# One weight ring for both phases of the FFNs and the mixing, with w2 in pieces of four feature blocks

## The chip, the cores and the metric

The kernel runs on one core of a Trainium2 chip. The metric is the device time of one execution in microseconds (us), as the median of several runs. The engines are TensorE (PE: matmuls, PEld: weight loads), VectorE (DVE), ScalarE (ACT), GpSimd (POOL) and SyncE (SP, which here issues nearly all DMAs).

## The reference, cut to what matters

One layer of a decoder trunk over 1104 tokens (16 meta, 1024 prompt, 64 sample) of width 1024, with a feed-forward width of 2816:

```python
def swiglu(x, w1, w3, w2):
    return (jax.nn.silu(x @ w1) * (x @ w3)) @ w2

x = x + 0.5 * swiglu(rmsnorm(x, ffn1_norm_g), ffn1_w1, ffn1_w3, ffn1_w2)
y, st = mix(rmsnorm(x, mix_norm_g), state, params)      # w_in, three recurrences, w_out
x = x + y
x = x + 0.5 * swiglu(rmsnorm(x, ffn2_norm_g), ffn2_w1, ffn2_w3, ffn2_w2)
out = rmsnorm(x, final_norm_g)
```

All is float32.

## The kernel before, in words

Every float32 operand of a matmul is split into a high part (a cast to a rounded float32 form, on ScalarE, L114) and a low part (the rest, on VectorE, L115). A product is three matmuls: high by high, high by low, low by high. Activations lie with features on the partitions, in 128-wide feature blocks, and tokens along the free axis. The helper that makes the two parts is `split`.

The program has these stages, in time order. FFN1, first phase (0 to 521 us): `group` (matmul L355) and `plain` (matmul L403) make the 22 blocks of the hidden vector from w1 and w3. Weights come as 128x4x256 raw tiles (`raw`, two buffers, pool r1, 4 KB a partition each) and as seven pairs of `whi` and `wlo` of 512 elements (pool w1). A finished hidden tile goes to DRAM (L413, L437). FFN1, second phase (521 to 825 us): the loop over THIRDS1 takes the tokens in three thirds of 336, 384 and 384 columns; for each it reads x into `xo` (L1567, one buffer), reads the 22 hidden blocks of those columns back (`hr`, L472, three buffers; the first third's come from tiles read earlier) and calls `third`. `third` runs over four pairs of output blocks and, inside, over pieces of w2: it loads a piece (L487), splits it, does its matmuls (L493) and at the end of a pair adds the result to x (L500). Pieces are of three feature blocks, the last two of two; raw, high and low tiles of w2 have two buffers each in a pool of their own. The mixing (825 to 1347 us): weights of w_in and w_out come through `wload` (load L188, matmul L198) in a pool "wp" of three buffers each for raw, high and low, 1024 elements at a time, 28 units; around them run the recurrences. The third block of w_out and the norms of FFN2 (1347 to 1420 us), where `wfetch` (L1620) loads w_out and L1638 multiplies. FFN2, first phase (1420 to 1899 us), as in FFN1. FFN2, second phase (1909 to 2180 us): the loop over THIRDS2, thirds of 320, 384 and 384 columns, with x from L1696 and w2 in pieces of 6, 6, 5 and 5 blocks (KQ). Then the last outputs are written.

The order on each engine and queue is set ahead of time by a scheduler that simulates the program; each engine and each DMA queue then works strictly in that order. Tiles rotate within their pools: a tile can be written when the last reader of the tile before it in the same buffer is done, and a pool's memory can be used by a later pool when its readers are done.

While the second phase of FFN1 begins, SP also issues the loads of the constants of the mixing (L1358 to L1447: wif, wtml, st, wkS, wvS, wqS and others) and the first loads of the mixing's weights.

## Time and profile before

| what | value |
|---|---|
| median of 3 runs | 2199.27 us (2198.92 to 2201.39) |
| the profiled execution | 2197.51 us, its span 2195.8 us |
| TensorE busy | 2091.2 us, 95% of the span |
| VectorE, ScalarE, GpSimd busy | 59%, 41%, 13% |
| mean granted TensorE clock | 0.977 |
| DMA | 275.47 MB, mean 125 GB/s |

The span is the time from the first to the last instruction that the profiler records. A granted clock of 1.00 is 2.4 GHz, 0.5 is 1.2 GHz. In a timeline a row that ends in [a <-b] had its engine idle for a us before it, and b is what ended that. The chain of work that ended last is followed back from the last instruction, and each of its pieces is what the next one waited for.

### The profile page before, as it was taken

The page shows a single profiled execution, that of the slowest core. Times are in us where ns is not written, and L with a number is a line of the kernel's source. Part 1 is how long each engine was busy: PE and PEld are TensorE (multiplying, and loading weights), DVE is VectorE, ACT ScalarE, POOL GpSimd, SP SyncE. Part 2 cuts the span into 40 slices and gives each one's busy share as a digit, 9 for nine tenths or more (in the row PEclk, how much of TensorE's full clock was granted, in tenths as well). Part 3 has the DMA queues.
Part 4 walks back from the last instruction along what each step waited for, and adds up shares of the span by engine and source line. Part 5 has one row for each costly group of instructions (what it writes and reads, how often), then busy time and mean ns, then how long its engine had stood idle before and what let it go on. Part 6 is the DMA issues. An engine that isn't in the chain of part 4 may idle for free.

```text
span 2195.8 us, 37582 instructions
## 1 busy us (share of the span) xinstructions
PE 2091.2 (95%) x14600; PEld 2040.3 (93%) x14600; DVE 1288.7 (59%) x2707; ACT 898.0 (41%) x1809; POOL 276.2 (13%) x284
## 2 busy tenths in 40 slices
PE   6999999998999999999998898999999999899997
PEld 6999999998989899978997797999999999899997
DVE  7765555562464535766687784767555556356343
ACT  5433232342353433635646663433233334244322
POOL 0222323211110001000000000004223221000000
PEclk8999999999999999999999999899999999899998
DMA  6322222244674633544344325432222223567342
GB/s 210 106 80 94 89 69 90 72 137 133 184 246 132 224 112 114 132 138 137 103 104 112 84 88 166 127 112 81 81 89 88 70 80 123 184 226 245 129 147 82
DMA packets 292743, 275.47 MB, mean 125 GB/s; under 512 B 46943, under 2 KB 277380, under 8 KB 292052
## 3 DMA queue, kind: packets, MB, share of 16 engines
q1 hardware_dynamic: 287772, 271.27, 39.5%
q10 hardware_dynamic: 4792, 1.78, 0.4%
q8 instruction: 115, 1.88, 0.3%
q14 instruction: 64, 0.52, 0.1%
HBM read 212.99 MB, written 60.01 MB: 124 GB/s over the span
## 4 chain that ended last, share of the span: by engine, by line
PE 82%; DMA 7%; DVE 5%; ACT 3%; SPq 1%; issue 1%; DVEq 0%; ACTq 0%
PE p L493 20%; PE b L355 14%; PE c L355 10%; PE a L355 9%; PE pw L198 9%; PE a L403 4%; PE b L403 4%; PE pwo L198 2%; DMA w<-in_ffn_w_dram 2%; PE pwo L1638 1%; DMA hr<-hidden 1%; PE pA L1029 1%; PE pq L827 1%; PE ssp L264 1%; DMA zg<-z_z 1%
## 5 line engine op out<-in xcount | busy, mean ns | idle before, releaser
L493 PE MATMUL p<-h,w2h 128*128 128x384 f32 (+2 forms) x2080 | 395.2, 332 | 32.6 <-ACT w2h L114 32.6
L493 PEld LDWEIGHTS p<-h,w2h 128*128 128x128 f32 x2080 | 352.8, 191 | 37.9 <-ACT w2h L114 37.3
L115 DVE TENSOR_TENSOR w2l<-w,w2h 128x768 fp32r<-128x768 f32 (+3 forms) x144 | 165.5, 1150 | 242.8 <-ACT w2h L114 239.3
L114 ACT CAST w2h<-w 128x768 fp32r<-128x768 f32 (+3 forms) x144 | 140.7, 978 | 313.4 <-PE p L493 193.3
L114 ACT CAST whi<-wraw 128x512 fp32r<-128x512 f32 (+1 forms) x216 | 143.6, 673 | 284.7 <-PE a L355 112.2
L355 PE MATMUL b<-op,whi 128*128 128x256 f32 (+2 forms) x1728 | 256.6, 289 | 0.3 <-DVE c L362 0.2
L355 PEld LDWEIGHTS b<-op,whi 128*128 128x128 f32 x1728 | 233.5, 188 | 1.0 <-DVE c L362 1.0
L115 DVE TENSOR_TENSOR wlo<-wraw,whi 128x512 fp32r<-128x512 f32 (+1 forms) x216 | 177.6, 828 | 83.0 <-ACT whi L114 77.9
L493 PE MATMUL p<-h,w2l 128*128 128x384 f32 (+2 forms) x1040 | 213.2, 330 | 0.0
L330 POOL TENSOR_TENSOR ws<-wraw 128x512 f32<-128x512 f32 x72 | 107.6, 1494 | 741.5 <-DMA wraw<-in_ffn_w_dram 610.0
L362 DVE TENSOR_TENSOR c<-p,b 128x256 f32<-128x256 f32 (+2 forms) x216 | 94.5, 438 | 172.0 <-PE b L355 158.7
L493 PEld LDWEIGHTS p<-h,w2l 128*128 128x128 f32 x1040 | 178.5, 190 | 0.0
L355 PE MATMUL c<-op,whi 128*128 128x256 f32 (+2 forms) x1152 | 172.4, 289 | 0.3 <-DVE op L115 0.3
L355 PE MATMUL a<-op,whi 128*128 128x256 f32 (+2 forms) x1152 | 171.6, 289 | 0.0
L355 PEld LDWEIGHTS c<-op,whi 128*128 128x128 f32 x1152 | 155.3, 189 | 0.5 <-DVE op L115 0.5
L355 PEld LDWEIGHTS a<-op,whi 128*128 128x128 f32 x1152 | 154.7, 189 | 0.0
L355 PE MATMUL b<-op,wlo 128*128 128x256 f32 (+2 forms) x864 | 144.3, 289 | 0.0
L114 ACT CAST whi<-ws 128x512 fp32r<-128x512 f32 x144 | 88.0, 618 | 135.1 <-PE b L355 83.4
L355 PEld LDWEIGHTS b<-op,wlo 128*128 128x128 f32 x864 | 122.4, 188 | 0.0
L115 DVE TENSOR_TENSOR wlo<-ws,whi 128x512 fp32r<-128x512 f32 x144 | 101.2, 703 | 2.1 <-PE b L403 1.7
L198 PE MATMUL pw<-sh,whi 128*128 128x384 f32 (+1 forms) x480 | 97.6, 338 | 0.2 <-DVE stg L571 0.2
L355 PE MATMUL a<-op,wlo 128*128 128x256 f32 (+2 forms) x576 | 96.3, 289 | 0.5 <-DVE wlo L115 0.5
(466 smaller groups left out, 3542.5 us busy)
## 6 DMA issues: line engine op xcount, KB each, us to landing
wraw<-in_ffn_w_dram SPq DMA_DIRECT2D x104, 512.0 KB
w<-in_ffn_w_dram SPq DMA_DIRECT2D x72, 384.0 KB
w<-in_ffn_w_dram SPq DMA_DIRECT2D x24, 768.0 KB
hr<-hidden SPq DMA_DIRECT2D x88, 192.0 KB
w<-in_ffn_w_dram SPq DMA_DIRECT2D x24, 640.0 KB
hidden<-h SPq DMA_DIRECT2D x36, 256.0 KB
wraw<-in_w_in_dram SPq DMA_DIRECT2D x16, 512.0 KB
wraw<-in_w_out_dram SPq DMA_DIRECT2D x16, 512.0 KB
```

The source lines that it names most:

```text
L114: S.copy(hi, x)
L115: V.tensor_tensor(lo, x, hi.bitcast(F32), OP.subtract)
L198: PE.matmul(p, wsl(ww, k), xsl(xx, k), start=i == 0, stop=i == tot - 1)
L264: PE.matmul(ss[:m, j : j + 1], q[:, o : o + m], ones[:, :1], start=k == j == 0, stop=k == 7, skip_group_check=True,)
L330: G.tensor_tensor(t, x, y, op)
L355: PE.matmul(t[:, :n], ww[:, k, :], xx[:, k, :], start=first and i == 0, stop=i == 11, skip_group_check=True,)
L362: V.tensor_tensor(out, x, t[:, :n], OP.add)
L403: PE.matmul(p, w[:, k, :], x[:, k, :], start=c == 0, stop=c == 23)
L493: PE.matmul(ps_[e], t[a][:, k, e * 128 : e * 128 + 128], hs[k0 + k][b], start=k0 == 0 and i == 0, stop=k0 + nk == NFB and i == 3 * nk - 1, ...
L827: PE.matmul(p[:96, h, :m], wt[:, kb, sl, 0:96], cm[:, kb, :m], start=i == 0, stop=i == len(ks) - 1)
L1029: PE.matmul(p[:, a], x[:, a], y[:, a], start=True, stop=True)
L1638: PE.matmul(p, u[k // 4][a][:, k % 4, :], ys[2][b][:, k, :], start=i == 0, stop=i == 23)
```

## The change

- One pool, "wp" in FFN1 and the mixing and "w3" in FFN2, holds two raw tiles of 128x4x256 and seven pairs of `whi` and `wlo` of 512 elements. Both phases of an FFN use it, and in FFN1 the pool stays for the mixing. The pools w1, r1, w2 and the mixing's own wp are gone.
- `third` loads w2 in pieces of four feature blocks (the sixth and last of a pair of output blocks has two) into a raw tile, and splits a piece as two pairs of two blocks. `wload` splits a unit as two pairs.
- `third` calls `fetch()` behind the load of the second piece: the x fetch and, in FFN2, the load of the final gain stand there. `xo` has two buffers in FFN1 (FFN2 had two already), `hr` five in FFN1 (FFN2 keeps three).
- Two staging tiles move to another pool, and the PSUM pools of the second phases are opened in the other order, which gives the w2 outputs other banks.

```diff
-KQ = [(0, 6), (6, 6), (12, 5), (17, 5)]
+KQ = [(0, 4), (4, 4), (8, 4), (12, 4), (16, 4), (20, 2)]
...
+    def wraw(pool):
+        return pool.tile([128, 4, 256], F32, tag="raw", name="wraw", bufs=2)
+
+    def wpair(pool):
+        return [pool.tile([128, 4, 128], F32R, tag=tag, name=tag, bufs=7) for tag in ("whi", "wlo")]
+
-    def wload(*parts, shape=[128, 8, 128]):
-        raw = P["wp"].tile(shape, F32, tag="raw", name="wraw")
+    def wload(*parts):
+        raw = wraw(P["wp"]).rearrange("p k f -> p (k f)").rearrange("p (k f) -> p k f", f=128)
...
-        hi = P["wp"].tile(shape, F32R, tag="whi", name="whi")
-        lo = P["wp"].tile(shape, F32R, tag="wlo", name="wlo")
-        split(hi, lo, raw)
-        return hi, lo
+        u = []
+        for c in range(2):
+            u.append(wpair(P["wp"]))
+            split(*u[c], raw[:, 4 * c : 4 * c + 4, :])
+        return [h for h, _ in u], [l for _, l in u]
...
-    def third(w2, hs, x, n, w2p, pq, kq, done):
+    def third(w2, hs, x, n, wp, pq, done, fetch):
...
-            for k0, nk in kq:
-                t = [
-                    w2p.tile([128, wk, 256], dt, tag=tag, name=tag, bufs=2)[:, :nk, :]
-                    for dt, tag in ((F32, "w2"), (F32R, "w2h"), (F32R, "w2l"))
-                ]
-                nc.sync.dma_start(t[0], wr[:, k0 : k0 + nk, d * 128 : d * 128 + 256])
-                split(t[1], t[2], t[0])
+            for k0, nk in KQ:
+                raw = wraw(wp)
+                nc.sync.dma_start(raw[:, :nk, :], wr[:, k0 : k0 + nk, d * 128 : d * 128 + 256])
+                t = []
+                for k in range(0, nk, 2):
+                    t.append([y.rearrange("p a f -> p (a f)").rearrange("p (k f) -> p k f", f=256) for y in wpair(wp)])
+                    split(*t[-1], raw[:, k : k + 2, :])
+                if d == 0 and k0 == KQ[1][0]:
+                    fetch()
...
+        P["wp"] = pool(front, "wp")
...
-        P["wp"] = front.enter_context(tc.tile_pool(name="wp", bufs=3, reuse_waits="tile"))
...
-            x = xq.tile([128, 8, 384], F32, tag="xo", name="xo")[:, :, :n]
-            nc.sync.dma_start(x, xin[:, :, c0 : c0 + n])
+            x = xq.tile([128, 8, 384], F32, tag="xo", name="xo", bufs=2)[:, :, :n]
             if b:
-                hs = hidden(hs_tile, 6, raw_each(hp, hd1, c0, n))
+                hs = hidden(hs_tile, 6, raw_each(hp, hd1, c0, n, 5))
...
-        oa = pool(ph, "oa3")
+        oa, wp = pool(ph, "oa3"), pool(ph, "w3")
...
-        pq, pz = pool(ph, "q4", 2, space=PSUM), pool(ph, "z4", 4, space=PSUM)
+        pz, pq = pool(ph, "z4", 4, space=PSUM), pool(ph, "q4", 2, space=PSUM)
```

Where the first phase of FFN1 ends, SP's queue read before (L413 stores hidden tiles, L487 loads w2 pieces, L1567 fetches x, L1360 to L1436 load constants, L472 loads hidden columns):

```order
L413 DMA hidden_76<-c 128x256
L389 DMA wraw<-in_ffn_w_dram 128x4x256
L413 DMA hidden_76<-c 128x256 x6
L1567 DMA xo<-xin 128x8x336
L487 DMA w_5967<-in_ffn_w_dram 128x3x256
L413 DMA hidden_76<-c 128x256
L487 DMA w_5991<-in_ffn_w_dram 128x3x256
L1360 DMA wif<-in_ml_w_if_dram 96x12x8
L1364 DMA wtml_wq<-in_ml_wq_dram 96x4x96
```

And now (L418 stores hidden tiles, L489 loads w2 pieces, L1584 fetches x):

```order
L396 DMA wraw<-in_ffn_w_dram 128x4x256
L418 DMA hidden_74<-c 128x256 x2
L489 DMA wraw<-in_ffn_w_dram 128x4x256
L418 DMA hidden_74<-c 128x256
L489 DMA wraw<-in_ffn_w_dram 128x4x256 x2
L418 DMA hidden_74<-c 128x256
L489 DMA wraw<-in_ffn_w_dram 128x4x256
L418 DMA hidden_74<-c 128x256 x2
L489 DMA wraw<-in_ffn_w_dram 128x4x256
L1584 DMA xo<-xin 128x8x336
L418 DMA hidden_74<-c 128x256
L1367 DMA wif<-in_ml_w_if_dram 96x12x8
```

Five loads of w2 stand ahead of the x fetch, where none stood before.

On ScalarE the same place read before (L408 evacuates `plain`, the casts are those of w1 and w3 and then of w2, which is named w2h):

```order
L114 CAST whi<-wraw 128x512 x4
L408 ACTIVATE c<-a 128x256
L114 CAST whi<-wraw 128x512
L408 ACTIVATE c<-b 128x256
L408 ACTIVATE c<-a 128x256
L408 ACTIVATE c<-b 128x256
L114 CAST w2h<-w_5967 128x768
```

And now (L413 evacuates `plain`; the casts behind the evacuation of a are of w2, but for the first one):

```order
L112 CAST whi<-wraw 128x512 x4
L413 ACTIVATE c<-a 128x256
L112 CAST whi<-wraw 128x512 x2
L413 ACTIVATE c<-b 128x256
L413 ACTIVATE c<-a 128x256
L112 CAST whi<-wraw 128x512 x2
L413 ACTIVATE c<-b 128x256
L112 CAST whi<-wraw 128x512 x6
```

Casts of w2 have moved between and ahead of the last evacuations of the first phase.

Where the first phase of FFN2 ends, SP's queue read before (L1674 loads the final gain, L1696 fetches x):

```order
L413 DMA hidden_14843<-c 128x256 x6
L1674 DMA gb<-in_final_norm_g_dram 128x1024
L1696 DMA xo<-xspill_0_72 128x8x320
L413 DMA hidden_14843<-c 128x256
L487 DMA w_21005<-in_ffn_w_dram 128x6x256
L487 DMA w_21047<-in_ffn_w_dram 128x6x256
L1696 DMA xo<-xspill_1_73 128x3072
L472 DMA hr<-hidden_14843 128x384 x3
```

And now (L1704 loads the final gain, L1702 fetches x, L477 loads hidden columns; one more w2 load stands just ahead of these rows):

```order
L489 DMA wraw<-in_ffn_w_dram 128x4x256 x2
L418 DMA hidden_15039<-c 128x256
L489 DMA wraw<-in_ffn_w_dram 128x4x256
L418 DMA hidden_15039<-c 128x256 x2
L489 DMA wraw<-in_ffn_w_dram 128x4x256
L477 DMA hr<-hidden_15039 128x384
L418 DMA hidden_15039<-c 128x256
L477 DMA hr<-hidden_15039 128x384 x2
L1702 DMA xo<-xspill_0_70 128x8x320
L1704 DMA gb<-in_final_norm_g_dram 128x1024
L1702 DMA xo<-xspill_1_71 128x3072
L489 DMA wraw<-in_ffn_w_dram 128x2x256
```

Here too the w2 loads come first, and the x fetches and the gain stand between the fifth and the sixth of them.

## Rows read from the trace of the kernel before

**Rows 1.** the page, part 1, TensorE: busy us (share of the span) and instructions

```profile
PE 2091.2 (95%) x14600; PEld 2040.3 (93%) x14600; DVE 1288.7 (59%) x2707; ACT 898.0 (41%) x1809; POOL 276.2 (13%) x284
```

**Rows 2.** page part 5, w2 matmuls: busy, mean ns, idle before, releaser

```profile
L493 PE MATMUL p<-h,w2h 128*128 128x384 f32 (+2 forms) x2080 | 395.2, 332 | 32.6 <-ACT w2h L114 32.6
```

**Rows 3.** the timeline of TensorE, first boundary of FFN1: start, us, instruction, count

```profile
527.01 3.73 PE L493 MATMUL p<-h,w2h 128*128 128x336 f32 x12 [6.42 <-ACT w2h L114]
530.53 1.88 PE L493 MATMUL p<-h,w2l 128*128 128x336 f32 x6
...
541.33 2.75 PE L493 MATMUL p<-h,w2h 128*128 128x336 f32 x12 [2.21 <-ACT w2h L114]
543.87 1.89 PE L493 MATMUL p<-h,w2l 128*128 128x336 f32 x6
...
571.80 2.11 PE L493 MATMUL p<-h,w2h 128*128 128x336 f32 x12 [1.29 <-ACT w2h L114]
```

**Rows 4.** the timeline of TensorE at the third boundaries of FFN1

```profile
618.94 1.50 PE L493 MATMUL p<-h,w2h 128*128 128x336 f32 x8 [0.63 <-ACT w2h L114]
...
636.22 2.37 PE L493 MATMUL p<-h,w2h 128*128 128x384 f32 x12 [1.66 <-ACT w2h L114]
...
725.09 0.44 PE L493 MATMUL p<-h,w2h 128*128 128x384 f32 x1 [1.38 <-ACT w2h L114]
...
748.41 2.37 PE L493 MATMUL p<-h,w2h 128*128 128x384 f32 x12 [0.88 <-ACT w2h L114]
```

**Rows 5.** the timeline of TensorE between the phases of FFN2

```profile
1909.26 6.22 PE L493 MATMUL p<-h,w2h 128*128 128x320 f32 x24 [10.34 <-ACT w2h L114]
...
1917.07 1.92 PE L493 MATMUL p<-h,w2h 128*128 128x320 f32 x12
```

**Rows 6.** the timeline of ScalarE behind the first boundary of FFN1

```profile
526.12 0.83 ACT L114 CAST w2h<-w 128x768 fp32r<-128x768 f32 x1 [16.50 <-DMA w<-in_ffn_w_dram]
...
539.28 1.04 ACT L114 CAST whi<-wraw 128x1024 fp32r<-128x1024 f32 x1 [3.25 <-DMA wraw<-in_w_in_dram]
...
549.60 0.62 ACT L114 CAST w2h<-w 128x512 fp32r<-128x512 f32 x1 [0.73 <-DMA w<-in_ffn_w_dram]
```

**Rows 7.** the chain that ended last, FFN1, first boundary: start, us, what

```profile
522.48 2.93 SPq L1364
...
532.85 6.41 DMA wraw<-in_w_in_dram
```

**Rows 8.** the chain that ended last, boundary to the third third of FFN1

```profile
717.63 2.60 DMA hr<-hidden
...
731.59 7.78 DMA w<-in_ffn_w_dram
```

**Rows 9.** the chain that ended last, between the phases of FFN2

```profile
1899.81 7.84 DMA w<-in_ffn_w_dram
```

**Rows 10.** windows: busy us of PE, PEld, DVE, ACT, POOL; clock, DMA share, GB/s

```profile
620.00:640.00 20.00, 17.23 (x101) 16.32 (x101) 14.37 (x30) 10.72 (x20) 2.41 (x2) 1.00 0.96 311
1160.00:1280.00 120.00, 100.37 (x698) 88.97 (x697) 91.19 (x367) 80.65 (x257) 3.88 (x10) 0.90 0.35 90
1900.00:1920.00 20.00, 10.74 (x56) 10.75 (x57) 6.64 (x6) 6.24 (x8) 0.00 (x0) 0.66 1.03 356
1920.00:1940.00 20.00, 20.00 (x139) 20.00 (x138) 12.87 (x17) 10.28 (x15) 0.00 (x0) 1.00 0.73 233
```

**Rows 11.** the timeline of TensorE, third block of W_out

```profile
1350.41 2.03 PE L1638 MATMUL pwo<-sh,whi 128*128 128x384 f32 x8 [3.30 <-ACT whi L114]
...
1367.55 1.65 PE L1638 MATMUL pwo<-sh,whi 128*128 128x384 f32 x4 [6.94 <-ACT whi L114]
```

**Rows 12.** the timeline of SP ahead of the third block of W_out

```profile
1344.33 1.18 SPq L1620 DMA_DIRECT2D wraw<-in_w_out_dram  x2
```

**Rows 13.** the timeline of TensorE in the mixing, 384 columns

```profile
829.61 1.55 PE L198 MATMUL pw<-sl,whi 128*128 128x384 f32 x8
831.00 1.55 PE L198 MATMUL pw<-sh,wlo 128*128 128x384 f32 x8
```

More of the change, by code (lines that the diff above doesn't have):

```diff
@@ L320, in weights @@
             for i in range(2):
-                t = rq.tile([128, 4, 256], F32, tag="raw", name="wraw", bufs=2)
+                t = wraw(wp)
                 src = w.rearrange("(k p) f -> p k f", p=128)
@@ L338, in weights @@
             for p, x in zip(ORDER, (a11, s2, a12, s3, s1, a22, s4)):
-                hi = wq.tile([128, 4, 128], F32R, tag="whi", name="whi", bufs=7)
-                lo = wq.tile([128, 4, 128], F32R, tag="wlo", name="wlo", bufs=7)
-                split(hi, lo, x)
-                u[p] = (hi, lo)
+                u[p] = wpair(wp)
+                split(*u[p], x)
             return u
@@ L386, in plain @@
                 for i in range(2):
-                    t = rq.tile([128, 4, 256], F32, tag="raw", name="wraw", bufs=2)
+                    t = wraw(wp)
                     src = A[ffn + "_w" + nm].rearrange("(k p) f -> p k f", p=128)
@@ L390, in plain @@
                     for g in range(2):
-                        hi = wq.tile([128, 4, 128], F32R, tag="whi", name="whi", bufs=7)
-                        lo = wq.tile([128, 4, 128], F32R, tag="wlo", name="wlo", bufs=7)
-                        split(hi, lo, t[:, :, g * 128 : g * 128 + 128])
-                        u.append((hi, lo))
+                        u.append(wpair(wp))
+                        split(*u[-1], t[:, :, g * 128 : g * 128 + 128])
                 for g in range(2):
@@ L1456, in tile_step @@
         st = ExitStack()
[L1457 to L1459 removed]
+        P["wp"] = pool(front, "wp")
+        tp, bp, xp, sq_, cp, o8, ob = (pool(st, n) for n in ("t1", "b1", "x1", "s1", "c1", "o81", "ob1"))
         pq, pz = pool(st, "q1", 2, space=PSUM), pool(st, "z1", 2, space=PSUM)
         xtile, norms, broadcast, normal, operands, plain, group, bank, pz_ = first_phase(
[L1462 removed]
+            "ffn1", PARTS1, hd1, P["wp"], tp, bp, xp, sq_, cp, o8, pq, pz
         )
+        vs1 = tp.tile([8, 128], F32, tag="vstage1", name="vstage1", bufs=1)
+        nc.sync.dma_start(vs1, A["ffn1_norm_g"].rearrange("(k p) -> k p", p=128))
         chunks = [[(0, 80)] + [(80 + 128 * j, 128) for j in range(4)], [(128 * j, 128) for j in range(4)]]
@@ L1575, in done @@
                     square(tp, x, b, k)
-            third(A["ffn1_w2"], hs, x, n, w2p, pq, [(0, 3), (3, 3), (6, 3), (9, 3), (12, 3), (15, 3), (18, 2), (20, 2)], done)
+            third(
+                A["ffn1_w2"], hs, x, n, P["wp"], pq, done, lambda: nc.sync.dma_start(x, xin[:, :, c0 : c0 + n])
+            )
             nc.sync.dma_start(xdr[b][:, :, :n], x)
@@ L1617, in wfetch @@
             wo = A["w_out"].rearrange("(k p) f -> p k f", p=128)
-            raw = rq.tile([128, 4, 256], F32, tag="raw", name="wraw", bufs=2)
-            raw = raw.rearrange("p k f -> p (k f)").rearrange("p (k f) -> p k f", f=128)
+            raw = wraw(wp).rearrange("p k f -> p (k f)").rearrange("p (k f) -> p k f", f=128)
             nc.sync.dma_start(raw, wo[:, :, d * 128 : d * 128 + 128])
@@ L1627, in wout2 @@
                 for c in range(2):
-                    hi = wq.tile([128, 4, 128], F32R, tag="whi", name="whi", bufs=7)
-                    lo = wq.tile([128, 4, 128], F32R, tag="wlo", name="wlo", bufs=7)
-                    split(hi, lo, raw[:, 4 * c : 4 * c + 4, :])
-                    u.append((hi, lo))
+                    u.append(wpair(wp))
+                    split(*u[c], raw[:, 4 * c : 4 * c + 4, :])
                 x = cp.tile([128, 576], F32, tag=f"c3{d % 2}", name="xw")[:, :384]
@@ L1670, in tile_step @@
         st.close()
-        tp, h1p, w2p, hp = (pool(ph, n) for n in ("t4", "h4", "w4", "r4"))
-        pq, pz = pool(ph, "q4", 2, space=PSUM), pool(ph, "z4", 4, space=PSUM)
+        tp, h1p, hp = (pool(ph, n) for n in ("t4", "h4", "r4"))
+        pz, pq = pool(ph, "z4", 4, space=PSUM), pool(ph, "q4", 2, space=PSUM)
         gb = tp.tile([128, 1024], F32, tag="gb", name="gb")
-        nc.sync.dma_start(gb, A["final_norm_g"].rearrange("(o d) -> o d", o=1).partition_broadcast(128))
         def h1_tile(i):
@@ L1695, in tile_step, with fetch @@
             x = tp.tile([128, 8, 384], F32, tag="xo", name="xo", bufs=2)[:, :, :n]
-            nc.sync.dma_start(x, xdr2[j][:, :, 16:336] if j == 0 else xdr2[j])
+            def fetch():
+                nc.sync.dma_start(x, xdr2[j][:, :, 16:336] if j == 0 else xdr2[j])
+                if j == 0:
+                    nc.sync.dma_start(gb, A["final_norm_g"].rearrange("(o d) -> o d", o=1).partition_broadcast(128))
             if j:
-                hs = hidden(*((h1_tile, 4) if j == 1 else (h2_tile, 6)), raw_each(hp, hd2, c0, n))
+                hs = hidden(*((h1_tile, 4) if j == 1 else (h2_tile, 6)), raw_each(hp, hd2, c0, n, 3))
             xt = [tp.tile([128, 1024], F32, tag=f"xt{i}", name="xt") for i in range(3)]
@@ L1705, in done @@
                     turn(j, x, 0, 4, xt, ss, 0)
-            third(A["ffn2_w2"], hs, x, n, w2p, pq, KQ, done)
+            third(A["ffn2_w2"], hs, x, n, wp, pq, done, fetch)
             turn(j, x, 4, 6, xt, ss, 1)
```

33 lines of the change are left out of this document (14 added, 19 removed).

## Prediction

> **What bounds the kernel now.** I read the busy table first. TensorE works for 95% of the span [rows 1], so time can only be saved where it stands still or runs at half clock, or by fewer matmuls, and the change leaves the matmuls as they are. Next the table of costly groups: the largest idle time on TensorE ahead of one line is 32.6 us in front of the w2 matmuls L493, and all of it ended when ScalarE finished a w2 cast [rows 2]. The timeline of TensorE says where these 32.6 us lie. Between the first phase of FFN1 and its second phase there are seven gaps, the first 6.42 us, the last 1.29 us, 14.1 us together [rows 3]. Four gaps stand where FFN1 goes from its first third of columns to its second (0.63 to 1.66 us, 3.4 together) and four where it goes to the third (1.38 to 0.88 us, 4.7 together) [rows 4]. One gap of 10.34 us stands between the phases of FFN2 [rows 5].
>
> After the long gaps the matmuls themselves are slow. In FFN1 the first twelve take 3.73 us where twelve of the same form later take 2.11 us [rows 3]: the granted clock is at its lower level, 1.2 GHz, after TensorE has stood still. In FFN2 the first 24 take 6.22 us where twelve later take 1.92 us [rows 5]. In that window of 20 us the mean granted clock is 0.66 and TensorE works for 10.74 us [rows 10].
>
> Then I asked what the gaps wait for. At 526.12 ScalarE had been idle for 16.50 us until a w2 piece landed [rows 6], and in FFN2 the w2 load was issued at 1899.81, after the last matmul of the first phase, and took 7.84 us [rows 9]. So the weights of the second phase are asked for only when the first phase ends. The next pieces wait on SP behind loads of constants, one of which holds the queue for 2.93 us [rows 7]. And ScalarE, which works in order, stood at 539.28 in front of a mixing weight that took 6.41 us to land, while w2 pieces queued behind that cast [rows 6, 7]. At the third boundaries the chain goes through loads of the hidden columns (2.60 us and alike, one after another) and then through a w2 load of 7.78 us [rows 8], with the DMA engines at a mean 0.96 of their time [rows 10].
>
> **The change, part by part.** *First boundary of FFN1.* By the order of the changed kernel, SP issues five w2 pieces of four blocks ahead of or between the last hidden stores, and the splits of the first two and most of the third wait for no matmul of the last quarter of the first phase's last block, so they can be done before it ends. The piece buffers are those of w1 and w3, so a piece needs no memory that the first phase still holds, and the output banks come from other tags. What goes away is 14.1 us of gaps and the half-clock loss. The latter: 18 matmuls of the first piece at 1.62/12 = 0.135 us too much each, 2.4 us, and in the second slow stretch 12 matmuls that take 2.75 for 2.11 us and 6 at the lower level, 0.6 + 0.8 us [rows 3]; together 3.8 us. Gross 17.9 us.
>
> What is late next is the refill. A matmul of 384 columns comes every 0.174 us [rows 13], so a piece of 24 matmuls keeps TensorE for 3.65 us at 336 columns, 3.5 at 320 and 4.2 at 384. Five pieces in hand are 18 us. The sixth load stands behind the x fetch, a store and eight loads of constants, some 7 us of issuing by the largest of them [rows 7]; with 6.4 to 7.8 us to land [rows 7, 8] and a cast of 0.62 [rows 6] it is ready some 15 us after the boundary, 3 us early. The ones behind it have about as much to spare. I take 1.5 us of new waiting, and 0 to 6 as bounds. The mixing weights now stand behind all of w2 on SP, so ScalarE can no longer stop in front of one.
>
> *Third boundaries.* The x fetch moves out of the boundary (a second buffer), five hidden columns are loaded ahead instead of three, and the split w2 reaches 3.5 pieces, 14 us, plus two raw pieces; before it was two pieces of three blocks. Gross 8.1 us [rows 4]. The traffic is the same and near its limit there [rows 10], so 1.5 us stay, bounds 0 to 5.
>
> *FFN2.* Five pieces are issued before the end of the first phase, then the two x fetches and the final gain, 3.4 MB, ahead of the sixth. Gross 10.34 us and 6.22 - 2 x 1.92 = 2.4 us of half clock [rows 5], 12.7 us. At the 356 GB/s of that window [rows 10] 3.4 MB with the w2 and hidden loads around them, 4.5 MB, take 12.6 us; the sixth piece is wanted after 5 x 3.5 = 17.5 us. At the 311 GB/s of the busiest third-boundary window [rows 10] they take 14.5 us and 3 us are to spare. I take 1.5 us, bounds 0 to 5.
>
> *More and smaller splits.* FFN2 had 48 casts of 1280 or 1536 elements and has 132 of 512; FFN1 had 96, and has 132; the mixing's 28 weight units take two casts each instead of one. A cast of 1024 takes 1.04 us, one of 512 takes 0.62 [rows 6], so each further cast is worth 0.20 us. In the second phases ScalarE is idle for half of the time (10.28 of 20 us busy [rows 10]) and 11 casts per 22 blocks are 6.8 us against at least 19 us of matmuls: free. In the mixing 28 x 0.20 = 5.6 us lie on an engine on which the recurrence also depends; where TensorE waits there (100.37 of 120 us busy [rows 10]) it waits for the recurrence. I take 0.5 us, bounds -5 to 5.6, the gain because this stage's order shifts a little and it has 20 us of waiting to move.
>
> The Trainium skill, "VectorE: DVE Perf Modes", section "The TRN2 errata — SBUF-src ops pay a fixed extra latency per instruction", states that ScalarE and VectorE pay a fixed latency for each instruction on SBUF operands, so that many small tiles pay it many times, and advises 512 elements or more. That speaks against this part of the change; the 0.20 us agree with it. By that rule alone, with nothing hidden in the mixing, the sum below would be 5.1 us worse.
>
> *Third block of W_out, after the mixing.* Its raw buffers lie in memory of the weight ring that is read until the last matmul of the mixing; before, they were free earlier and the load went out at 1344.33 [rows 12], 2.8 us before TensorE ran dry; the gap was 3.30 us [rows 11]. Now the load goes out 2.8 us later. But the next gap, 6.94 us to 1367.55 [rows 11], waits for loads behind a fixed row of sixteen x loads, and shrinks by what the first grows. I take 1 us, bounds 0 and 3.
>
> The sum: 17.9 + 8.1 + 12.7 = 38.7 us gross, less 1.5 + 1.5 + 1.5 + 0.5 + 1.0 = 6.0, is 32.7 us. The profiled run of 2197.5 us would become 2164.8. The median of the runs shown stands 1.8 us above that run, so 2166.6; I say **2166 us**.
>
> **The rivals.** *(a) The refill only moves the wait.* There are two raw buffers, so two pieces can be fetched per landing. If loads land in 7.8 us [rows 8], two pieces take 7.8 + 1.2 of casts + 0.7 for the subtraction (an estimate from the cast) + 0.4 of issue = 10.1 us, 5.1 a piece against 3.5 to 4.2 of matmuls. Eight pieces at the first boundary lose 11 us less 4 in hand, six at each third boundary 5.4 less about half, six in FFN2 9.6 less 4: 18 us instead of 4.5, and the time is 2180. For it: 0.96 and 1.03 of DMA time at these places [rows 10]. Against: such landings last for one or two pieces, and the lead is 3.5.
>
> *(b) Small splits in the mixing are not hidden.* All 5.6 us show: 2172 us. It is the page's rule above as a rival. Against: TensorE is busy for most of the mixing.
>
> *(c) Slower than before: the ring is too short for the mixing.* Its weights have two raw and 3.5 split buffers where they had three of each. If each of the 28 units waits for its load, 1.66 us like the longest gap of a third boundary [rows 4], 46 us are lost, and the time is 2212. It decides from 32.7 / 28 = 1.2 us per unit. Against: a unit is 48 or 72 matmuls of up to 0.174 us, 8 to 12 us, and a load takes 4 to 8 us in all, so one unit of lead is enough and there are two.
>
> *(d) It does not do what it says.* If the pieces' splits waited for pairs that the first phase's last matmuls still read, the casts would start at the boundary again and only the thirds could gain, with the longer weight ring for that: 2190 to 2199, about no change. The order says otherwise, for the reason given above.
>
> **How the numbers follow.** Forecast with its bounds, about 2156 to 2176: 0.62; (b) 0.10; (a) 0.14; (c) 0.06; (d) 0.04; better than all bounds together, with a gain in the mixing, 0.04. The likeliest gives 2166. The low end is nothing left at any boundary and 3 us from the mixing: 2197.5 + 1.8 - 38.7 - 3 = 2157.6, and I go to 2156. The upper end takes (b) and most of (a): 2187. A measurement of this kernel can tell 0.2%, 4.4 us, from no change. Faster than that 0.90, within it 0.03, slower 0.07: (c) and a piece of (d).
>
> **What would show it.** TensorE's timeline should go from the last L403 matmul to the first w2 matmul with no gap worth naming in either FFN, and the granted clock should stay at its upper level there. The idle time before the w2 matmuls should fall from 32.6 to about 5 us, and what is left should be named a w2 cast waiting for its load, some 15 to 30 us after a boundary. The first w2 casts of 0.62 us should start before the last L403 matmul. The gap before the third block of W_out should be near 6 us and the next one shorter. I am wrong if the 32.6 us turn up at later pieces, if waiting in the mixing grows, or if matmuls of the same form take longer, which nothing here excludes since all buffers move.

## The result, and the profile after

| | median of the runs | profiled run, span |
|---|---|---|
| before | 2200.56 us (2198.92 to 2201.39) | 2195.8 us |
| after | 2178.35 us (2172.91 to 2179.83) | 2177.3 us |

The ratio of the times is 0.9896, with a 95% interval of 0.9881 to 0.9910. Measured twice more beside the kernel before it was 0.9884 [0.9859, 0.9910] and 0.9885 [0.9871, 0.9900]. The change makes the kernel 22 to 26 us faster. That is two thirds of the 33 us that were forecast.

Stage by stage, with each border set at the end of a stage's last matmul, worked out from the two traces (length / idle time of TensorE / time at half clock, us):

| stage | before | after | difference in length |
|---|---|---|---|
| FFN1, first phase | 520.6 / 18.6 / 13.7 | 521.5 / 17.3 / 17.1 | +0.9 |
| FFN1, second phase | 304.1 / 22.2 / 10.2 | 284.0 / 7.9 / 6.8 | -20.1 |
| mixing | 522.4 / 24.0 / 23.9 | 529.3 / 25.2 / 34.1 | +6.9 |
| third block of W_out, norms | 74.3 / 13.2 / 27.3 | 74.7 / 12.9 / 30.7 | +0.4 |
| FFN2, first phase | 477.5 / 1.2 / 0 | 476.4 / 1.1 / 0 | -1.1 |
| FFN2, second phase | 280.1 / 10.3 / 13.7 | 274.6 / 4.1 / 6.8 | -5.5 |
| last outputs | 16.7 / 15.3 / 11.4 | 16.8 / 15.4 / 10.9 | +0.1 |

Both second phases got shorter, and the mixing got longer. How far one trace can be trusted: the second phase of FFN1 took 304.1 and 309.6 us in two traces of the kernel before and 284.0, 283.0 and 281.9 in three of the kernel after, and that of FFN2 280.1 and 279.4 against 274.6, 275.5 and 274.6. Three readings explain most of it.

**The wait for w2 is gone.** These are the busy row of TensorE on the page of the kernel after, and the group of the w2 matmuls, which were L493 and are now L500. They answer to [rows 1, 2]:

```profile
PE 2093.9 (96%) x14600; PEld 2043.4 (94%) x14600; DVE 1297.4 (60%) x2855; ACT 911.0 (42%) x1957; POOL 274.4 (13%) x284
...
L500 PE MATMUL p<-h,whi 128*128 128x384 f32 (+2 forms) x2080 | 399.7, 330 | 0.8 <-ACT whi L112 0.8
```

The idle time ahead of the w2 matmuls went from 32.6 us to 0.8. On TensorE's timeline at the two phase boundaries (start, length, line, operation; idle before and its releaser in brackets, where there was any; [rows 3, 5] are the same places before), first FFN1 and then FFN2:

```profile
520.88 0.64 PE L408 MATMUL b<-op,wlo 128*128 128x256 f32 x4
521.36 1.41 PE L500 MATMUL p<-h,whi 128*128 128x336 f32 x8
522.61 0.77 PE L500 MATMUL p<-h,wlo 128*128 128x336 f32 x4
...
1885.28 0.62 PE L408 MATMUL b<-op,wlo 128*128 128x256 f32 x4
1885.74 1.33 PE L500 MATMUL p<-h,whi 128*128 128x320 f32 x8
```

There is no gap in either, and eight matmuls of 336 columns take 1.41 us, at a granted clock of 1.00 (first row of the windows below). ScalarE around the boundary of FFN1:

```profile
519.65 0.62 ACT L112 CAST whi<-wraw 128x512 fp32r<-128x512 f32 x1 [3.69 <-PE b L408]
521.08 0.62 ACT L112 CAST whi<-wraw 128x512 fp32r<-128x512 f32 x1 [0.81 <-PE b L408]
524.32 0.62 ACT L112 CAST whi<-wraw 128x512 fp32r<-128x512 f32 x1 [2.62 <-PE p L500]
```

The cast at 524.32 is the first that waits for a w2 matmul, that is, for the first w2 pair to come free. The ring has seven pairs, so the seven casts before it, the last of which starts at 521.08, were all of w2. In the table of windows (window, TensorE, weight loads, VectorE, ScalarE and GpSimd busy, each with its instructions, then granted clock, DMA share, GB/s) the 20 us after the boundary are full:

```profile
521.00:541.00 20.00, 20.00 (x134) 20.00 (x133) 4.70 (x17) 4.93 (x10) 8.47 (x35) 1.00 0.75 228
...
600.00:620.00 20.00, 12.69 (x77) 12.37 (x75) 13.59 (x24) 12.82 (x28) 2.14 (x2) 0.92 0.87 288
...
619.00:622.00 3.00, 2.99 (x12) 2.99 (x13) 3.00 (x8) 1.36 (x3) 0.00 (x0) 0.50 1.00 293
...
1972.00:1975.00 3.00, 2.10 (x9) 1.54 (x9) 2.57 (x6) 2.17 (x7) 0.00 (x0) 0.50 0.82 266
```

The first of these rows shows the gain. The second shows where a part of it went back, and the last two the granted clock at its lower level behind the two gaps that come next.

**A new wait at the first third boundary.** In the stretch from 600 to 620 TensorE works for 12.69 of 20 us. Its timeline there, and at the first third boundary of FFN2:

```profile
603.90 1.55 PE L500 MATMUL p<-h,whi 128*128 128x384 f32 x8
...
610.14 1.55 PE L500 MATMUL p<-h,whi 128*128 128x384 f32 x8
619.01 1.28 PE L156 MATMUL ssp<-ones,acc 128*80 128x1 f32 x6 [7.31 <-POOL acc L148]
620.15 1.63 PE L500 MATMUL p<-h,wlo 128*128 128x384 f32 x4
621.58 2.46 PE L500 MATMUL p<-h,whi 128*128 128x384 f32 x8
...
1972.90 0.42 PE L1693 MATMUL xps<-ident,xo 128*64 128x128 f32 x1 [3.61 <-DVE xo L507]
1972.97 0.99 PE L500 MATMUL p<-h,whi 128*128 128x384 f32 x2
1976.37 2.58 PE L500 MATMUL p<-h,whi 128*128 128x384 f32 x8
```

It is not w2 that is late. In FFN1 the wait is in front of the six small matmuls `ssp` (L156), which sum the squares of the finished third for the norm. In FFN2 it is in front of one transpose `xps` (L1693) of the finished third. TensorE works in order, so the ready w2 matmuls of the next third stand behind them. After the gap eight matmuls of 384 columns take 2.46 and 2.58 us instead of 1.55: the granted clock is 0.50 from 619 to 622 us and from 1972 to 1975 us. The two waits are there in each of the three traces of this kernel, 7.31, 6.05 and 6.08 us in front of `ssp` and 3.61, 5.67 and 4.05 us in front of `xps`.

Why are the squares late? Here are ScalarE and VectorE in that stretch:

```profile
614.03 0.51 ACT L112 CAST h<-hr 128x384 fp32r<-128x384 f32 x1 [3.01 <-DMA hr<-hidden]
...
615.86 0.47 ACT L147 ACTIVATE sq<-xo 128x336 f32<-128x336 f32 x1
...
614.57 0.56 DVE L113 TENSOR_TENSOR h<-hr,h 128x384 fp32r<-128x384 f32 x1 [2.49 <-ACT h L112]
615.05 0.50 DVE L507 SCALAR_TENSOR_TENSOR xo<-p,xo 128x336 f32<-128x336 f32 x1
```

ScalarE stands for 3.01 us at the split of a hidden column tile of the *next* third (`h<-hr`), which has not landed. VectorE stands at 614.57 at the other half of that split. Behind it is the last addition to x of the *finished* third (L507 at 615.05), and behind that come the squares (L147) and their sum on GpSimd (L148). The chain of waits puts it in one line:

```profile
598.70 5.67 DMA hr<-hidden
...
607.26 6.74 DMA hr<-hidden
...
617.11 0.47 ACT sq L147
...
617.72 1.25 POOL acc L148
619.01 1.28 PE ssp L156 x6
```

In the kernel before, the last additions of the third ran 2 us after the first matmul of the next third, which starts at 624.28, and `ssp` came without a wait:

```profile
626.23 0.91 DVE L500 SCALAR_TENSOR_TENSOR xo<-p,xo 128x336 f32<-128x336 f32 x2
...
631.86 0.68 PE L158 MATMUL ssp<-ones,acc 128*80 128x1 f32 x6
```

In the kernel after, the next third starts at 603.90 and the last addition runs at 615.05, 11 us later.

**The third block of W_out** came as forecast. SP issues its first loads after the last matmul of the mixing, which ends at 1334.77; the gaps are 4.45 and 5.50 us instead of 3.30 and 6.94 [rows 11, 12]. What SP waited for (us in total, times, longest), and the SP and TensorE timelines:

```profile
SPq L1627 <- PE pwo L207: 2.9, 1, 2.9
...
1334.81 1.01 SPq L1627 DMA_DIRECT2D wraw<-in_w_out_dram  x2
...
1339.22 2.93 PE L1643 MATMUL pwo<-sh,whi 128*128 128x384 f32 x8 [4.45 <-ACT whi L112]
...
1355.37 1.65 PE L1643 MATMUL pwo<-sh,whi 128*128 128x384 f32 x4 [5.50 <-ACT whi L112]
```

### The profile page after: what moved, and what is told of

It reads as the page before. It is cut to its first block, busy times and chain, and to the rows that moved or that the text cites. A ratio compares the mean times of both kernels' runs of the same rounds, so it can differ in the third digit from the quotient of the medians.

```text
span 2177.3 us, 38160 instructions
## 1 busy us (share of the span) xinstructions
PE 2093.9 (96%) x14600; PEld 2043.4 (94%) x14600; DVE 1297.4 (60%) x2855; ACT 911.0 (42%) x1957; POOL 274.4 (13%) x284
## 4 chain that ended last, share of the span: by engine, by line
PE 85%; DMA 5%; DVE 5%; ACT 3%; issue 1%; SPq 1%; POOL 0%; DVEq 0%; ACTq 0%; POOLq 0%
PE p L500 22%; PE b L362 15%; PE c L362 10%; PE a L362 9%; PE pw L207 9%; PE a L408 4%; PE b L408 4%; PE pwo L207 3%; DMA wraw<-in_ffn_w_dram 1%; PE pwo L1643 1%; PE pq L834 1%; PE pA L1036 1%; PE ssp L273 1%; DMA hr<-hidden 1%; DVE wlo L113 1%
## 5 line engine op out<-in xcount | busy, mean ns | idle before, releaser
L113 DVE TENSOR_TENSOR wlo<-wraw,whi 128x512 fp32r<-128x512 f32 x508 | 360.0, 727 | 333.1 <-ACT whi L112 237.6
L112 ACT CAST whi<-wraw 128x512 fp32r<-128x512 f32 x508 | 302.0, 618 | 566.8 <-PE p L500 154.0
L500 PE MATMUL p<-h,whi 128*128 128x384 f32 (+2 forms) x2080 | 399.7, 330 | 0.8 <-ACT whi L112 0.8
L500 PEld LDWEIGHTS p<-h,whi 128*128 128x128 f32 x2080 | 352.2, 189 | 3.1 <-ACT whi L112 2.8
L500 PE MATMUL p<-h,wlo 128*128 128x384 f32 (+2 forms) x1040 | 220.8, 329 | 0.0
L500 PEld LDWEIGHTS p<-h,wlo 128*128 128x128 f32 x1040 | 179.2, 189 | 0.0
L207 PE MATMUL pw<-sh,wlo 128*128 128x384 f32 (+1 forms) x480 | 98.2, 340 | 0.0
L369 DVE TENSOR_TENSOR c<-c 128x256 f32<-128x256 f32 (+2 forms) x144 | 62.8, 436 | 58.1 <-PE c L362 57.7
```

Source lines behind the costliest of these rows:

```text
L112: S.copy(hi, x)
L113: V.tensor_tensor(lo, x, hi.bitcast(F32), OP.subtract)
L207: PE.matmul(p, wsl(ww, k), xsl(xx, k), start=i == 0, stop=i == tot - 1)
L369: V.tensor_tensor(out, x, t[:, :n], OP.add)
L500: PE.matmul(ps_[e], t[k // 2][a][:, k % 2, e * 128 : e * 128 + 128], hs[k0 + k][b], start=k0 == 0 and i == 0, stop=k0 + nk == NFB and i == ...
```

## The experiments

Times of different chips are compared only through the ratio to the kernel before, which ran on the same chip. The stage lengths are those of the table above, for each kernel's own trace.

**1. Weight ring, but not shared (e4_noshare).** The kernel after, with pools of their own for the second phases, opened when the first phase has ended:

```diff
-        P["wp"] = pool(front, "wp")
-        tp, bp, xp, sq_, cp, o8, ob = (pool(st, n) for n in ("t1", "b1", "x1", "s1", "c1", "o81", "ob1"))
+        wp1, tp, bp, xp, sq_, cp, o8, ob = (pool(st, n) for n in ("w1", "t1", "b1", "x1", "s1", "c1", "o81", "ob1"))
...
         P["big"] = pool(front, "big")
+        P["wp"] = pool(front, "wp")
...
-        tp, h1p, hp = (pool(ph, n) for n in ("t4", "h4", "r4"))
+        tp, h1p, wp, hp = (pool(ph, n) for n in ("t4", "h4", "w4", "r4"))
```

> One part undone: the second phases get a ring of the same size of their own, in memory that the first phase gives back at its end, so the sharing is gone; pieces, fetch places, hidden buffers and banks stay as in the changed kernel. Theory E (the gain at the phase boundaries comes from pieces loaded and split in buffers that the first phase frees early): the gap between the phases is back, 6 us or more in FFN1 and 8 us or more in FFN2, with half-clock time behind it, and the time is 15 to 30 us above the changed kernel. Rival F (the later x fetch and the other banks bring most of it): gaps under 3 us and less than 8 us above.

Measured: 2217.28 us, ratio 1.0031 [1.0015, 1.0046]. The kernel is slower than before. The gaps at the phase boundaries are back, in FFN1 one and in FFN2 two large ones, as TensorE's timeline shows:

```profile
538.03 4.25 PE L500 MATMUL p<-h,whi 128*128 128x336 f32 x16 [14.21 <-ACT whi L112]
...
1915.34 2.62 PE L500 MATMUL p<-h,whi 128*128 128x320 f32 x16 [3.15 <-ACT whi L112]
...
1929.04 1.17 PE L500 MATMUL p<-h,whi 128*128 128x320 f32 x3 [6.39 <-ACT whi L112]
```

All else of the change is in this kernel: the pieces of four, the ring, the two x buffers, the five hidden columns, the moved fetch. So none of these closes the gaps at the phase boundaries without the sharing, by which pieces are loaded and split while the first phase still runs. The second phases take 298.9 and 289.0 us, 14.9 and 14.4 more than in the kernel after; the mixing is longer too, at 536.9 us. In ratio the sharing is worth 1.0031 - 0.9896 = 0.0135, some 30 us, all this together.

The waits at the third boundaries are there as well, though TensorE comes to them later than in the kernel after (to `ssp` 107.5 us after the end of the first phase, against 90.2):

```profile
636.46 0.85 PE L156 MATMUL ssp<-ones,acc 128*80 128x1 f32 x4 [5.10 <-POOL acc L148]
...
2012.95 0.42 PE L1693 MATMUL xps<-ident,xo 128*64 128x128 f32 x1 [5.31 <-DVE xo L507]
```

**2. Three hidden column buffers (e1_hr3).** The kernel after with the old number in FFN1:

```diff
-                hs = hidden(hs_tile, 6, raw_each(hp, hd1, c0, n, 5))
+                hs = hidden(hs_tile, 6, raw_each(hp, hd1, c0, n, 3))
```

> One part undone: three buffers for hidden columns in FFN1 instead of five. Theory A1 (five buffers let the scheduler put more hidden splits ahead of the last adds to x, so the deeper prefetch itself makes the 7.31 us gap): the gap at the first third boundary shrinks below 3 us and the time falls by 4 us or more. Rival A2 (the splits wait for landings of 6 to 7 us, and fewer buffers only make the chain of landings longer): the gap stays or grows, and waits for hidden columns come back ahead of L500, as in the kernel before; the time rises by 0 to 8 us.

Measured: 2188.80 us, ratio 0.9907 [0.9884, 0.9931], not to be told from the change; the 4 us of theory A1 did not come. But the waits sit elsewhere:

```profile
552.68 1.71 PE L500 MATMUL p<-h,whi 128*128 128x336 f32 x8 [1.39 <-ACT whi L112]
...
559.87 2.47 PE L500 MATMUL p<-h,whi 128*128 128x336 f32 x8 [3.02 <-ACT whi L112]
...
622.05 1.28 PE L156 MATMUL ssp<-ones,acc 128*80 128x1 f32 x6 [3.13 <-POOL acc L148]
```

The wait in front of `ssp` shrinks from 7.31 to 3.13 us, and 4.4 us of waiting for w2 appear 29 and 37 us after the phase boundary, which is at 523.2. The chain that leads to the second of these goes through loads of constants that SP issues one after the other from 548.70 to 554.06 (L1365), with the w2 load behind them landing in 3.92 us. The norm itself came no sooner: `ssp` starts 98.9 us after the phase boundary, and 97.5, 95.6 and 95.3 us after it in the three traces of the change. TensorE only came to it later. So five hidden buffers alone don't make the wait.

**3. The norm's small matmuls later (e2_late, e5_late2, e6_late_ffn2).** If in-order engines make the norm late, small matmuls that stand later in TensorE's queue should cost nothing. In e2_late those of a third are emitted at the second pair of output blocks of the next third, in both FFNs:

```diff
+            if d == 2 and late:
+                late()
             for k0, nk in KQ:
...
-            rstd_bc(tp, b)
+            late1 = lambda b=b: rstd_bc(tp, b)
+            if b == 2:
+                late1()
```

> The norm of a third (the ones matmuls L156 in FFN1, the output transposes L1693 and what follows them in FFN2) is written at the third pair of output blocks... of the next third instead of right behind its own; all else as in the changed kernel. Theory A (the two new gaps of 7.31 and 3.61 us stand only because TensorE's queue holds these small matmuls 40 to 48 matmuls behind the boundary, while the last adds to x wait on VectorE behind splits of hidden columns whose loads are late): both gaps go, with the half-clock time behind them (about 2 and 3 us), about 16 us less than the changed kernel, near 2162 us. Rival B (the DMA engines are full at these places and TensorE would wait for hidden columns or w2 pieces anyway): the waiting moves to the w2 matmuls L500 and the time stays within 5 us of 2178.

Measured: 2183.58 us, ratio 0.9879 [0.9856, 0.9901], where the change is; the 16 us of theory A did not come. Both gaps are gone, and others stand nearby:

```profile
613.12 0.34 PE L1387 MATMUL pg<-wif,wtml_wq 96*96 96x8 f32 x2 [4.18 <-ACT wtml_wq L1378]
...
2002.17 1.11 PE L1698 MATMUL xps<-ident,xo 128*128 128x128 f32 x4 [4.55 <-ACT xt L1699]
```

The first is a small matmul of the mixing's constants, whose input ScalarE copies behind the same splits. The second is again a transpose, whose output bank ScalarE frees behind a w2 cast that waits for its load. That the gaps went with the matmuls shows the mechanism, but more small matmuls stood in the same danger, and the third block of W_out and its norms took 80.0 us, 3 to 5 more than in the change. So e5_late2 also moves the constants' matmuls to the second pair of the second third, and in FFN2 goes to the third pair (`d == 4`):

```diff
-            rstd_bc(tp, b)
-            if b == 0:
-                consts = mixing_constants(K, tmp)
+            def late1(b=b):
+                rstd_bc(tp, b)
+                if b == 0:
+                    consts.extend(mixing_constants(K, tmp))
```

> As the run with the late norms, and the small matmuls of the mixing's constants also moved behind the first pair of output blocks of the second third; in FFN2 the rest of a third's output is moved behind the second pair of the next third. Theory A, widened (any small matmul that stands in TensorE's queue within 10 us of a third boundary and depends on ScalarE or VectorE waits there for the loads of hidden columns and w2 that these engines stand in front of; further away there is no such wait): no gap over 1 us in the second phases, the second phase of FFN1 about 276 us and that of FFN2 about 269 us, 10 to 14 us less than the changed kernel together. Rival B2 (the waits only move on to wherever the small matmuls stand): gaps of 4 us or so turn up again and the time stays within 5 us of the changed kernel.

Measured: 2187.49 us, ratio 0.9903 [0.9880, 0.9926]. At the third boundaries no gap over 1 us is left in either FFN, and the second phase of FFN2 takes 271.2 us; beside it on that chip the change took 275.5. But the total is no better, and the second phase of FFN1 takes 283.0 us, as in the change on that chip, where 276 were expected. A new gap opened after the first boundary of FFN1. TensorE's row, and the end of the chain that leads there:

```profile
554.56 4.85 PE L502 MATMUL p<-h,whi 128*128 128x336 f32 x16 [5.73 <-ACT whi L112]
```

```profile
541.89 0.36 SPq L1367
...
549.54 0.47 SPq L1367
...
550.11 3.70 DMA wraw<-in_ffn_w_dram
...
553.89 0.63 ACT whi L112
```

From 541.89 to 550.01 SP issues loads of constants one after the other (L1367), and the w2 load (L491) stands behind them, as in e1_hr3. That is rival (a) of the prediction, by way of SP's queue. The mixing also grew, from 528.9 to 535.5 us.

What was good in it was the part in FFN2. e6_late_ffn2 takes that alone, so FFN1 and the mixing stay as the change has them:

```diff
+            if d == 4 and late:
+                late()
             for k0, nk in KQ:
...
-            third(A["ffn2_w2"], hs, x, n, wp, pq, done, fetch)
+            third(A["ffn2_w2"], hs, x, n, wp, pq, done, fetch, late2)
+            late2 = lambda a=(j, x, chunks, s0, *xs): finish(*a)
+            if j == 2:
+                late2()
```

> The changed kernel, with the small matmuls and outputs of a third of FFN2 moved to the fifth and sixth output blocks of the next third; FFN1 and the mixing untouched. Theory A (in-order engines in front of late hidden columns make the norm late, and with it the small matmul in TensorE's queue): the gap at the third boundary of FFN2 goes, the second phase of FFN2 takes 271 instead of 275 us, everything else stays, and the time falls by 3 to 5 us, a ratio 0.0014 to 0.0023 below that of the changed kernel beside it. Rival (the wait only moves to the next small matmul or to the w2 pieces): 275 us again and the same time.

> The changed kernel once more, beside the next three on one chip. Ratio to the kernel before 0.988 to 0.990, as in the two measurements so far. The mixing with the third block of W_out near 605 us, the first third boundary of FFN2 with a gap of 3.6 to 5.7 us before the small matmul of the norm.

Measured on one chip: the change 2179.20 us, ratio 0.9885 [0.9871, 0.9900]; e6_late_ffn2 2172.43 us, ratio 0.9858 [0.9839, 0.9878]. The second phase of FFN2 falls from 274.6 to 269.2 us, with 1.1 us of idle time and none at half clock. TensorE where a third ends, and where the transposes now stand:

```profile
1964.74 1.55 PE L502 MATMUL p<-h,whi 128*128 128x384 f32 x8
...
2035.68 1.47 PE L1695 MATMUL xps<-ident,xo 128*128 128x128 f32 x12
2036.90 1.64 PE L502 MATMUL p<-h,whi 128*128 128x384 f32 x8
```

The twelve transposes run in 1.47 us without a wait. The stage accounts for 5.4 of the 6.8 us between the two medians. The two intervals overlap, so the times alone don't show a gain; the stage does, at 269.2 us against 274.6, 275.5 and 274.6 in the three traces of the change. Its median is the lowest here. The theory holds for FFN2: the wait was the norm's place in the queue. The wait in FFN1 (5.26 us in this trace) was not taken away without cost by any kernel here.

**4. What made the mixing longer.** First, whether it is real. The kernels before and after again, on one chip:

> The kernel before again, on the same chip as the three others of this group, so that its stages can be compared with theirs. If the times of single stages belong to the kernel (theory K), the mixing and the third block of W_out together take about 597 us as in the first profile; if they belong to the chip or to the single execution (theory L), they differ from that by 5 us or more.

> The changed kernel again, on the same chip. By theory K the mixing and the third block of W_out take about 604 us, 7 more than in the kernel before on this chip; by theory L the difference between the two is not 7 us here. The gaps of 7.31 us behind the first third boundary of FFN1 and 3.61 us behind that of FFN2 should be there again within 1 us.

Measured: before 2207.28 us, ratio 0.9994 [0.9978, 1.0009]; after 2183.76 us, ratio 0.9884 [0.9859, 0.9910]. The mixing and the third block of W_out together take 596.7 and 599.2 us in the two traces of before, and 604.0, 605.6 and 604.2 in the three of after. The 5 to 9 us are there each time. The two gaps came back as 6.05 and 5.67 us, so both missed the 1 us that was allowed.

Then each part of the mixing's change alone, put into the kernel before. The ring with its small splits (e3_mixring, and again on another chip as e3b_mixring):

```diff
-        raw = P["wp"].tile(shape, F32, tag="raw", name="wraw")
-        hi = P["wp"].tile(shape, F32R, tag="whi", name="whi")
-        lo = P["wp"].tile(shape, F32R, tag="wlo", name="wlo")
-        split(hi, lo, raw)
+        raw = P["wp"].tile([128, 8, 128], F32, tag="raw", name="wraw", bufs=2)
+        u = []
+        for c in range(2):
+            u.append([P["wp"].tile([128, 4, 128], F32R, tag=t, name=t, bufs=7) for t in ("whi", "wlo")])
+            split(*u[c], raw[:, 4 * c : 4 * c + 4, :])
```

> One part alone: the kernel before, with only the mixing's weights changed to two raw buffers and seven pairs of 512 elements. The mixing took 522.4 us before and 529.3 us in the changed kernel. Theory C (the smaller splits and the shorter ring cost the mixing these 6.9 us): about 529 us for the mixing here and 2207 us in all. Rival D (the mixing lost because its instructions were put in another order and left TensorE at the lower clock for longer, which any shift of the order can do): the mixing takes 522 us give or take 4, and the time stays near 2200.

> The kernel before with the mixing's weights in two raw buffers and seven pairs of 512 elements, once more, on the same chip as the kernel before and the changed one. Theory C (the smaller splits and the shorter ring cost the mixing time): the mixing and the third block of W_out take 5 us or more longer than in the kernel before on this chip. Rival D (they cost nothing, and what the mixing loses in the changed kernel comes from the order of its instructions): no longer than in the kernel before, give or take 3 us.

Only the splits in halves, in buffers as before (e7_halfcast), and only two raw buffers instead of three (e8_raw2):

```diff
-        split(hi, lo, raw)
+        for c in (0, 4):
+            split(hi[:, c : c + 4, :], lo[:, c : c + 4, :], raw[:, c : c + 4, :])
```

```diff
-        raw = P["wp"].tile(shape, F32, tag="raw", name="wraw")
+        raw = P["wp"].tile(shape, F32, tag="raw", name="wraw", bufs=2)
```

> The kernel before, with each weight unit of the mixing split in two halves of 512 elements, in its own three buffers of 1024. Theory B (the 28 further casts and subtractions cost the mixing its 6 to 7 us): mixing and third block of W_out together 602 to 605 us instead of 597 to 599, ratio 1.002 to 1.003. Theory O (only the order moves, no price of its own): within 3 us of 598, ratio 0.998 to 1.001.

> The kernel before, with two raw buffers for the weights of the mixing instead of three, nothing else. Theory R (the shorter ring makes units late): gaps before the weight matmuls of the mixing that end with a cast waiting for its load, mixing and third block of W_out together over 602 us, ratio above 1.002. Theory O (only the order moves): no such gaps, within 3 us of 598, ratio 0.998 to 1.001; the load of the third block of W_out may go out earlier, and its gap shrink.

Measured:

| kernel | ratio to before | mixing, us | third block of W_out, us | together |
|---|---|---|---|---|
| before, two traces | 1 | 522.4, 523.2 | 74.3, 76.0 | 596.7, 599.2 |
| splits in halves | 0.9977 [0.9968, 0.9986] | 519.1 | 73.3 | 592.4 |
| two raw buffers | 0.9964 [0.9950, 0.9978] | 521.1 | 77.5 | 598.6 |
| ring and splits | 0.9983 [0.9967, 0.9998] | 531.2 | 63.2 | 594.4 |
| the same, again | 0.9968 [0.9948, 0.9989] | 532.9 | 62.6 | 595.5 |
| after, three traces | 0.9896, 0.9884, 0.9885 | 529.3, 528.9, 529.0 | 74.7, 76.7, 75.2 | 604.0, 605.6, 604.2 |

Not one of the parts costs time. Half splits and two raw buffers alone make the kernel a little faster, more than either theory had said. The ring lengthens the mixing by 8 to 10 us, a little more than the change does, but gets it back in the next stage, where the change does not. The rows of SP and TensorE of e3b_mixring show how:

```profile
1345.84 2.93 SPq L1624 DMA_DIRECT2D wraw<-in_w_out_dram  x2
...
1358.91 1.55 PE L202 MATMUL pwo<-sh,wlo 128*128 128x384 f32 x8
1360.30 1.58 PE L1642 MATMUL pwo<-sh,whi 128*128 128x384 f32 x8
```

There the loads of the third block go out 14.5 us before the mixing's last matmul ends, and W_out follows without a gap. In after they go out at 1334.81, when that matmul has ended. SP stood in front of them for 2.9 us, waiting for that matmul, as the row above says; the rest is their later place in SP's queue. That the memory which FFN2's ring takes over from the mixing sets both, and so keeps the change from getting the time back, fits these traces but is not shown. In e4_noshare, which has the mixing's ring in another place, the loads go out at 1358.28, only 1.4 us before the mixing's last matmul ends, and the two stages take 610.0 us.

Why the ring lengthens the mixing at all is open, but the traces say where. The mixing's weight matmuls take 320.6 and 320.8 us in the two traces of before and 320.8, 320.8 and 320.5 in the three of after, counted from one start to the next and without the waits over 0.15 us. The small matmuls between them, of the recurrences for the most part, take 178.3 and 178.7 us before and 183.9, 183.9 and 183.0 after. So some 5 of the 6 to 7 us lie in these; the waits over 0.15 us grow by 0.5 to 2 us. The half clock does not explain it: the three traces of after have 34.1, 30.7 and 23.9 us of it in mixings of 529.3, 528.9 and 529.0 us.

## Why the prediction was right, and where it was not

The sum was to take 32.7 us off the profiled run, and the spans differ by 18.5. The 14.2 us that are missing are 3.8 in FFN1, 4.6 in FFN2 and 6.4 in the mixing, less 0.6 at the third block of W_out. The measured 2178.35 us lie above the 2156 to 2176 that the forecast with its bounds was given 0.62 for. They lie inside the whole range because its upper end of 2187 made room for rivals (a) and (b), and neither of these came in the change itself; that the total fits is in part luck.

*What bounds the kernel, and the phase boundaries: right.* The 32.6 us of [rows 2] were the weights of the second phase asked for too late, as [rows 6, 9] were read, and the half clock behind the gaps went with them. e4_noshare shows that it is the early loading that does it. Seven casts, three and a half pieces, start before the first w2 matmul at 521.36, somewhat more than the two pieces and most of a third that the prediction read from the order. So rival (d) falls.

*The refill: 1.5 us each time was too much, but the care was right.* 0.8 us is left in all of both FFNs. Rival (a) did not come in the change itself. It came in e1_hr3 (4.4 us) and e5_late2 (1.2 and 5.7 us) as soon as the order moved a little, in the longest gap of each with the w2 load behind constants on SP, a place for which the prediction had counted about 3 us to spare.

*The third boundaries: here the working failed.* The prediction asked "what is late next" of w2 alone. It counted the 8.1 us as won and left 1.5 for traffic. It did not ask what else TensorE has in its queue there. `ssp` and `xps` stand among the w2 matmuls of the next third, their inputs come from VectorE and ScalarE, and in front of those inputs stand splits of hidden columns that land in 5.67 and 6.74 us at a place with 0.87 of DMA time. In FFN1 that cost 7.31 us and at least 1.7 at half clock (2.46 for 1.55 and 1.63 for 0.86 us), 9.0 of the 26.0 us gross. 17.0 would be left; the measured gain of both phases is 19.2, and the 2 us between them are less than two traces of the same kernel differ. In FFN2 3.61 us of waiting and 2.3 at half clock (0.99 for 0.51, 1.63 for 0.85, 2.58 for 1.55) take 5.9 of the 12.7, and 6.8 should be left; 6.6 were measured. e6_late_ffn2 gives back 5.4 us of this by moving the small matmuls alone.

In the kernel before these matmuls did not wait. Whether its waits for w2 had given them time is open. For it: after the end of the first phase of FFN1 TensorE came to `ssp` in 111.3 us before and in 90.2 after, where the sums were ready in 97.5; and in e1_hr3 4.4 us of earlier waits take 4.2 off this one. Against it: in e4_noshare, where the waits at the phase boundaries are back, TensorE comes to `ssp` in 107.5 us and still waits 5.10. What the traces do show is a change of order: in FFN1 the last addition ran 2 us after the start of the next third, and now runs 11 us after it. Which part of the change moved it no run shows; e1_hr3 takes away two of the hidden buffers, and the wait for the norm stays.

*Splits and the ring in the mixing: the size was off.* Forecast 0.5 us with bounds -5 to 5.6, measured 6.9, so the bounds were too narrow. The prediction named a shift of the order, but only as a gain. Rival (b), the price of small casts, falls: e7_halfcast has all 28 further casts and is not slower. The Trainium skill, "VectorE: DVE Perf Modes", section "The TRN2 errata — SBUF-src ops pay a fixed extra latency per instruction", says that many small tiles pay a fixed latency many times. The 0.20 us a cast of [rows 6] agree, but e7_halfcast shows that in this stage nobody waits for them. Rival (c) falls too: in the three traces of after no weight matmul of the mixing waits 0.3 us or more for a weight's cast (the longest wait in front of one, 2.05 us, is for an activation), and with two raw buffers alone (e8_raw2) the ratio is below 1. What remains is the order of the small matmuls, which is not shown: the 5 us lie in them, and no kernel here changes their order alone. With the weights handled in five ways in the table, the mixing takes anything from 519.1 to 532.9 us.

*The third block of W_out: right against the kernel before* (+0.4 us for +1), with the two gaps as forecast. But in e3b_mixring, with the old kernel's other pools, the ring has 12 to 13 us less in that stage, which a comparison with the old trace alone could not show.

## What to carry to other kernels

When a transfer is taken off an engine's path, list everything that stands in that engine's queue at the same place, and for each entry what its producers are queued behind. An entry whose producers stand behind a late load is the next to be late, whatever the transfer was. Small matmuls of a norm whose result nobody needs soon can be emitted many matmuls later, which brought 5.4 us in FFN2 here; in FFN1 it brought no time, since other waits opened beside it. In a stage that waits on recurrences a change of buffers shifted 3 us one way and 10 the other here, and its bounds should be taken that wide.

## What the runs showed of the hardware that was not expected

- Half clock in a stage that waits anyway does not show in its length: 34.1, 30.7 and 23.9 us at half clock in three traces of one kernel, and 529.3, 528.9 and 529.0 us of mixing.
- A wait of 3.61 us in front of one transpose was followed by the lower clock level at once (granted clock 0.50 from 1972 to 1975 us), and eight matmuls took 2.58 us instead of 1.55: the price of the gap was 5.9 us in all.
- A hidden column tile of 192 KB took 5.67 and 6.74 us to land in a stretch with a DMA share of 0.87, and 2.60 us in [rows 8].
- The same kernel before had medians of 2200.56, 2208.55, 2208.13 and 2205.57 us beside the four groups of runs, 0.4% apart, which is as much as some of the effects looked for. Only ratios within a group tell them apart.
